# Spreading the adaLN row sums differently over the two passes of a SwiGLU's second matrix

## The chip, the cores and the metric

The kernel runs on one core of one Trainium2 chip. The metric is the device time of one execution in microseconds; the median of three timed runs of the kernel before is 2384.79 us (2383.39 to 2386.68).

## What is computed

Two layers, each a macaron block: a SwiGLU half step (FFN), a mixing step (attention, a chunked gating MLP and pooling), and a second FFN. That makes six stages: 0, 2, 3 and 5 are FFNs, 1 and 4 mix. Each stage ends with a gated residual and leads into a modulated norm; gate, scale and shift are the adaLN rows, each one a vector times a 1024 x 1024 slice of `w_mod`.

```python
def adaln(cvec, w_mod_l, b_mod_l):
    m = jax.nn.silu(cvec) @ w_mod_l + b_mod_l
    return m.reshape(cvec.shape[0], N_MOD, D_MODEL)
def ffn_half(x, mod, j, g_pre, g_post, w1, w2):
    h = modulate(rms_norm(x, g_pre), mod, j)
    return x + 0.5 * mod[:, j + 2][:, None, :] * rms_norm(swiglu(h, w1, w2), g_post)
```

There are 640 tokens (512 latent, 128 context), D_MODEL = 1024, D_FF = 2816, all in float32; context and latent tokens have their own conditioning vector, so every adaLN row is computed for two vectors.

## The kernel before, in words

**Precision.** Every operand of a large matmul is split into a rounded high part (ScalarE copy) and a low part (VectorE subtraction), and a product is three matmuls: hi x hi, lo x hi, hi x lo. For weights this is line 329 (`whi`, ScalarE) and line 331 (`wlo`, VectorE), for activations of the second matrix lines 765 (`ahi`) and 766 (`alo`).

**Tiles.** The five token tiles of 128 are in two groups: group A has tiles 0 and 1, group B tiles 2, 3 and the context tile 4. `ffn1` and `ffn1_blocks` compute the first matrix; its results are `act[f, g]` for 22 slices f of 128 hidden columns. `ffn2` computes the second matrix in two passes: the first pass for group A, the second for group B. A pass goes through 22 slices f and two output halves, that is 44 weight units of 128 x 512; each is loaded by a DMA on SyncE's queue (line 283, tile `raw`, five buffers) and split. The second pass keeps the last four units of the first and loads 40. In `mm_tok` (line 700) a unit yields 650 ns of nominal time per tile: 44 x 2 x 650 ns = 57.2 us for the first pass, 44 x 3 x 650 ns = 85.8 us for the second. The last four slices of a first pass are done tile by tile, so that tile 0 is complete before the pass ends. The products of tiles 0 and 1 stand in PSUM banks 4 to 7, those of tiles 2, 3 and 4 in banks 0 and 1, 2 and 3, 4 and 5.

**Boundary.** After a pass, `boundary` (`bnd_steps`, line 489) closes the stage for its tiles: square sums (ScalarE, 498), product with the gate row `mdG` (VectorE, 499), residual (509, or 506 in the last stage), norm (512), scale and shift rows (517 on VectorE, 520 on GpSimd), eight transposes a tile (528) and splits for the next stage (361, 362). Group A's boundary runs beside the second pass, group B's beside the start of the next stage. In stage 5 it ends at 506 and writes the output.

**adaLN rows.** `ada` (line 418) computes a list of rows in the background. A row takes a zeroed tile with the bias (`wb`, GpSimd 424, DMA 425), eight loads of 512 KB of `w_mod` (line 431, tile `wmt`, three buffers shared with `wb` and `gr`), for each of these two VectorE operations on 128 x 1024 (line 436, one for each conditioning vector, 16 a row), four DMAs of `norm_w` (442), four matmuls with ones that add over the partitions (445; the trace shows eight records), one operation that scales (449, 451 or 453), and four DMAs that write the row to DRAM (457). `load_md` (460) reads it back later, spread over all partitions. `rows(n)` gives the rows that the end of stage n wants: its gate G, and for the next stage S and T; stage 5 wants a gate alone. A row's yields are 8 x (300 + 2 x 1150) + 1700 = 22.5 us of nominal time.

**What sets the order.** The program is written as generators. `run` (122) and `beside` (137) step a main generator and let a background generator advance by a rate times the main one's nominal time. So a rate is a share of nominal time, and it fixes where in the order of the program the row's operations stand; `behind` moves them back by 30 places of priority. A scheduler then orders each engine's instructions by priority and a simulated timeline; on the chip each engine and each DMA queue works through its list in that order.

Stage s runs the rows of `ADA_LATE[s]` in its second matrix, in both passes at `ADA_RATE2`. In stage 0 six more rows run earlier, beside `ffn1`; that part is not touched.

```python
ADA_LATE = {0: (2,), 2: (3,), 3: (4, 5), 5: ()}
ADA_RATE2 = 0.7
...
            bg = ada(rows[1])
            run(self.ffn2(l, i, 0), (bg, ADA_RATE2))
            self.rings(ada=(7,))
            self.second_pass(s, last, self.ffn2(l, i, 1, last), bg)
```

`ffn2` splits activations with `ensure` (756): the first slice before its first matmul, then two slices ahead. The tiles come from pool `asp`, which in stages 2, 3 and 5 (`BLOCKS`) is opened only after `ffn1_blocks`, in memory that the tiles `SZ` of those blocks held.

Of the kernel before, what the change touches and what calls it, by code (L numbers as in the profile page):

```python
# [8 lines left out]
F32 = mybir.dt.float32  # L9
F32R = mybir.dt.float32r  # L10
# [5 lines left out]
P = 128  # L16
D = 1024
KD = 8
FF = 2816
NF = 22  # L20
# [5 lines left out]
WA = 256  # L26
# [4 lines left out]
ADA_LAG = 30  # L31
ADA_RATE = 0.65

ADA_LATE = {0: (2,), 2: (3,), 3: (4, 5), 5: ()}
ADA_RATE2 = 0.7

BLOCKS = (2, 3, 5)
S_LAG, S_RATE = 400, 0.45
# [112 lines left out]
def drain(*gens):  # L151
    for g in gens:
        for _ in g:
            pass
# [7 lines left out]
class Builder:  # L162
    def __init__(self, ctx, tc, a, n_stage=6):
# [32 lines left out]
        self.rowd = {}  # L196
        self.pairs = {}
        self.gap = None
        self.kept_tmp = {}

    def bank(self, i):
# [498 lines left out]
    def mm_tok(self, key, tiles, order, stat, late=0, tail=1):  # L700
# [18 lines left out]
        while ci < n:  # L719
# [25 lines left out]
                    yield 650 * len(tiles)  # L745
            ci += 1

    def ffn2(self, l, i, g, last=False):
        wid = (WA, WB)[g]
        sp = {}  # L750

        order = list(range(NF))
        if g:
            order = order[NF - KEEP_C:] + order[:NF - KEEP_C]

        def ensure(f):
            while len(sp) <= min(f, NF - 1):
                q = order[len(sp)]
                hi = self.asp.tile([P, WB], F32R, name="ahi")
                a = self.act[q, g]  # L760
                if len(sp):
                    lo = self.ap.tile([P, wid], F32, name="alo", tag=f"act{g}{order[len(sp) - 1]}").bitcast(F32R)
                else:
                    lo = self.asp.tile([P, WB], F32R, name="ahi")[:, 0:wid]
                self.nc.scalar.activation(hi[:, 0:wid], a, AF.Copy)  # L765
                self.nc.vector.tensor_tensor(lo, a, hi[:, 0:wid].bitcast(F32), ALU.subtract)  # L766
                sp[q] = (hi, lo)

        def stat(f):
            ensure(order.index(f) + 2)  # L770
            return sp[f]
        ensure(0)
        yield from self.mm_tok(lambda c, n: ("w2", l, i, c, n), (GA, GB)[g], order, stat, late=1 if g else 0, tail=(TAIL_A, TAIL_B, TAIL)[g + last])
# [523 lines left out]
    def ffn_stage(self, s, l, i, pend):  # L1297
# [8 lines left out]
        with tc.tile_pool(name="gap", bufs=1, reuse_waits="tile") as gp, tc.tile_pool(name="actp", bufs=1, reuse_waits="tile") as ap, ExitStack() as late:  # L1306
# [19 lines left out]
            if s in BLOCKS:  # L1326
                with tc.tile_pool(name="sp", bufs=2, reuse_waits="tile") as sp:
# [7 lines left out]
                    run(self.ffn1(l, i, early[-1:], (1,)))  # L1335
                    self.sum_in_place()
                    self.rings(acc=(0, 1, 2, 3, 4, 5, 6, 7))
                    run(self.ffn1_blocks(l, i, range(na, NF)))
            if s in BLOCKS:
                pools()  # L1340
            ada = lambda rows: behind(tc, self.ada(rows, block(self.wmp, "wmt"), block(self.accsp, "acc")), ADA_LAG)
# [12 lines left out]
                self.load_md(kind, s)  # L1354
            self.rings(ada=(3,))
            bg = ada(rows[1])
            run(self.ffn2(l, i, 0), (bg, ADA_RATE2))
            self.rings(ada=(7,))
            self.second_pass(s, last, self.ffn2(l, i, 1, last), bg)
            for t in (3, 4):  # L1360
# [3 lines left out]
    def second_pass(self, s, last, mm, bg=None):  # L1364
        q = STG[s]
        if bg:
            mm = beside(mm, bg, ADA_RATE2)
        b = self.boundary(s, GA, True, not last, 1, q["skew_a"])
        next(b)
        next(b)  # L1370
# [84 lines left out]
```

## Time and profile before

| | before |
|---|---|
| median of three runs | 2384.79 us |
| the profiled execution's own time | 2385.23 us |
| span of the profile | 2383.5 us |
| PE, DVE, ACT, POOL busy | 97%, 77%, 47%, 17% of the span |
| granted TensorE clock, mean | 0.993 of 2.4 GHz |

PE is TensorE's matmul stream, PEld its weight loads, DVE VectorE, ACT ScalarE, POOL GpSimd, SPq the DMA queue of SyncE. Busy shares are means over stages with different limits; matmul records overlap, so how long a stretch took says more than how busy PE was in it. An instruction's duration is longer than its share of a full engine, since the next one starts before it ends.

### The profile page before, as it was taken

To read this page: it belongs to the slowest core of one execution; us is meant where nothing else is said; L and a number is where in the kernel's file an instruction comes from. 1 tells how busy PE (TensorE), PEld (TensorE's weight loads), DVE (VectorE), ACT (ScalarE), POOL (GpSimd) and SP (SyncE) were. 2 spreads that over 40 slices of the span, in tenths; PEclk is the share of its full clock that TensorE was granted. 3 is DMA by queue.
4 is the path that set the end of the run, shared out by engine and by line. 5 is a ranking of instruction groups with operands and counts; after the bars stand their busy time and mean duration, and the time that the engine had idled before them with its cause. 6 is when DMAs were issued, how large, how long until landed. Compare 5 with 4: busy or idle time off the path is not lost.

```text
span 2383.5 us, 37305 instructions
## 1 busy us (share of the span) xinstructions
PE 2300.2 (97%) x13304; PEld 2050.9 (86%) x13304; DVE 1827.1 (77%) x2914; ACT 1118.5 (47%) x2309; POOL 393.5 (17%) x432
## 2 busy tenths in 40 slices
PE   8999999999999999998999999999999989999998
PEld 6999897787778899996789999877777779999887
DVE  5568678977686788889976888899867674888754
ACT  5422224444776344454443444444555553444543
POOL 2000000305324200000240000020645360000000
PEclk9999999999999999999999999999999999999999
DMA  9457657644325522247653322667621354232542
GB/s 295 117 174 244 200 189 261 232 157 137 98 72 168 160 85 84 80 160 248 222 181 120 89 86 75 212 227 244 204 74 63 106 173 134 75 89 71 187 158 93
DMA packets 330481, 360.07 MB, mean 151 GB/s; under 512 B 20451, under 2 KB 239843, under 8 KB 330294
## 3 DMA queue, kind: packets, MB, share of 16 engines
q1 hardware_dynamic: 326694, 344.58, 45.5%
q10 hardware_dynamic: 3600, 13.11, 1.4%
q8 instruction: 104, 1.70, 0.3%
q14 instruction: 83, 0.68, 0.1%
HBM read 341.50 MB, written 16.12 MB: 150 GB/s over the span
## 4 chain that ended last, share of the span: by engine, by line
PE 71%; DVE 13%; DMA 6%; issue 5%; POOL 2%; ACT 2%; SPq 1%; DVEq 0%; ACTq 0%; POOLq 0%
PE PS L366 69%; DVE wlo L331 3%; DMA wmt<-in_w_mod 3%; DVE acc L436 3%; DMA raw<-in_ffn_w 2%; DVE alo L766 1%; PE PS L445 1%; POOL tmp L520 1%; DVE ast L1063 1%; DVE x L509 1%; PE PS L1086 1%; DVE tl L362 1%; DVE h1lo L362 1%; POOL wlo L331 1%; ACT whi L329 0%
## 5 line engine op out<-in xcount | busy, mean ns | idle before, releaser
L329 ACT ACTIVATE whi<-raw 128x512 fp32r<-128x512 f32 x668 | 416.5, 630 | 525.5 <-PE PS L366 379.5
L331 DVE TENSOR_TENSOR wlo<-raw,whi 128x512 fp32r<-128x512 f32 x614 | 455.2, 755 | 198.7 <-ACT whi L329 190.0
L366 PE MATMUL PS<-whi,ahi 128*128 128x512 f32 x920 | 353.6, 392 | 0.0
L366 PE MATMUL PS<-h1hi,whi 128*128 128x384 f32 (+1 forms) x1016 | 341.5, 337 | 6.4 <-ACT h1hi L361 6.4
L366 PE MATMUL PS<-h1lo,whi 128*128 128x384 f32 (+1 forms) x1016 | 344.6, 339 | 0.0
L366 PE MATMUL PS<-wlo,ahi 128*128 128x512 f32 x880 | 342.7, 391 | 0.0
L366 PE MATMUL PS<-h1hi,wlo 128*128 128x384 f32 (+1 forms) x1016 | 341.8, 336 | 0.0
L329 ACT ACTIVATE whi<-tmp 128x512 fp32r<-128x512 f32 x294 | 185.7, 633 | 244.6 <-PE PS L366 175.3
L436 DVE SCALAR_TENSOR_TENSOR acc<-wmt,ccs,acc 128x1024 f32<-128x1024 f32 x224 | 279.9, 1279 | 26.8 <-DMA wmt<-in_w_mod 26.7
L366 PE MATMUL PS<-h0hi,whi 128*128 128x256 f32 x1016 | 287.3, 284 | 7.6 <-DVE act L602 7.4
L366 PE MATMUL PS<-whi,alo 128*128 128x512 f32 x840 | 272.7, 395 | 21.2 <-DVE alo L766 20.9
L366 PE MATMUL PS<-h0hi,wlo 128*128 128x256 f32 x1016 | 285.4, 282 | 0.0
L366 PE MATMUL PS<-h0lo,whi 128*128 128x256 f32 x1016 | 285.3, 281 | 0.0
L331 DVE TENSOR_TENSOR wlo<-tmp,whi 128x512 fp32r<-128x512 f32 x294 | 201.7, 687 | 77.5 <-ACT whi L329 71.4
L366 PEld LDWEIGHTS PS<-whi,alo 128*128 128x128 f32 x840 | 155.3, 188 | 66.6 <-DVE alo L766 30.0
L366 PEld LDWEIGHTS PS<-h0hi,whi 128*128 128x128 f32 x1016 | 193.5, 191 | 18.4 <-DVE act L602 8.8
L366 PEld LDWEIGHTS PS<-whi,ahi 128*128 128x128 f32 x920 | 173.8, 189 | 39.1 <-ACT ahi L765 1.7
L366 PE MATMUL PS<-sz,whi 128*128 128x384 f32 x784 | 199.3, 335 | 0.0
L366 PEld LDWEIGHTS PS<-h0hi,wlo 128*128 128x128 f32 x1016 | 193.6, 191 | 4.3 <-issue 3.4
L366 PEld LDWEIGHTS PS<-h1hi,whi 128*128 128x128 f32 x1016 | 190.7, 188 | 7.0 <-ACT h1hi L361 7.0
L366 PEld LDWEIGHTS PS<-wlo,ahi 128*128 128x128 f32 x880 | 166.2, 189 | 34.7
L366 PEld LDWEIGHTS PS<-h0lo,whi 128*128 128x128 f32 x1016 | 193.9, 191 | 1.8 <-issue 1.7
(239 smaller groups left out, 4204.6 us busy)
## 6 DMA issues: line engine op xcount, KB each, us to landing
raw<-in_ffn_w SPq DMA_DIRECT2D x540, 256.0 KB
wmt<-in_w_mod SPq DMA_DIRECT2D x136, 512.0 KB
tmp<-in_ffn_w SPq DMA_DIRECT2D x98, 512.0 KB
raw<-in_w_in SPq DMA_DIRECT2D x80, 256.0 KB
xd<-x ACTq DMA_DIRECT2D x25, 512.0 KB
x<-xd SPq DMA_DIRECT2D x25, 512.0 KB
raw<-in_w_out SPq DMA_DIRECT2D x64, 128.0 KB
mdG<-rowG SPq DMA_DIRECT2D x12, 512.0 KB
```

The source lines that it names most:

```text
L329: self.nc.scalar.activation(hi, r, AF.Copy)
L331: eng.tensor_tensor(lo, r, hi.bitcast(F32), ALU.subtract)
L362: i1 = (eng or self.nc.vector).tensor_tensor(lo, src, hi.bitcast(F32), ALU.subtract)
L366: self.nc.tensor.matmul(out, w, m, start=start, stop=stop)
L436: nc.vector.scalar_tensor_tensor(accs[s], w, self.cc[:, s, k:k + 1], prev, ALU.mult, ALU.add)
L445: nc.tensor.matmul(ps[32 * q:32 * q + 32, :], self.ones[:, 0:32], accs[q // 2][:, 512 * (q % 2):512 * (q % 2) + 512], start=True, stop=Tru ...
L509: nc.vector.scalar_tensor_tensor(x, tmp, r, x, ALU.mult, ALU.add)
L520: nc.gpsimd.tensor_tensor(tmp[:, hs], tmp[:, hs], self.md["T", st][:, hs], ALU.add)
L766: self.nc.vector.tensor_tensor(lo, a, hi[:, 0:wid].bitcast(F32), ALU.subtract)
L1063: nc.vector.tensor_reduce(mx, S, AX.X, ALU.max)
L1086: nc.tensor.transpose(ps[:, w * c + P * j:w * c + P * j + P], pt[:, n * j + P * (c0 + c):n * j + P * (c0 + c) + P], self.ident)
```

## The change

Three edits. First, the two passes get rates of their own: 0.3 in the first and 0.62 in the second pass of stages 0, 2 and 3 in place of 0.7 in both. Second, the one row of stage 5 (its gate) moves from the end of stage 3's list into stage 5's own first pass, at rate 0.5; what is left of it is issued when that pass is written out, and then its two `load_md` DMAs. Third, in stages 2, 3 and 5 the high and low parts of group A's slices 0 and 1 are made ahead of the last slice of `ffn1_blocks`, into a tile of the `tmp` pool, and `ffn2` takes them from there.

```diff
-ADA_LATE = {0: (2,), 2: (3,), 3: (4, 5), 5: ()}
-ADA_RATE2 = 0.7
+ADA_LATE = {0: (2,), 2: (3,), 3: (4,), 5: (5,)}
+ADA_RATES = {0: (0.3, 0.62), 2: (0.3, 0.62), 3: (0.3, 0.62), 5: (0.5, 0.62)}
...
+    def split_first(self):
+
+        t = self.tmpp.tile([P, D], F32, name="first", tag="tmp").bitcast(F32R)
+        self.early = {}
+        for f in range(2):
+            hi, lo = (t[:, 512 * f + WA * n:512 * f + WA * n + WA] for n in range(2))
+            self.split(hi, lo, self.act[f, 0])
+            self.early[f] = (hi, lo)
+
     def ffn2(self, l, i, g, last=False):
         wid = (WA, WB)[g]
         sp = {}
+        if g == 0 and self.early:
+            sp, self.early = self.early, {}
...
-                    run(self.ffn1_blocks(l, i, range(na, NF)))
+                    run(self.ffn1_blocks(l, i, range(na, NF - 1)))
+                    self.split_first()
+                    run(self.ffn1_blocks(l, i, range(NF - 1, NF)))
...
-            run(self.ffn2(l, i, 0), (bg, ADA_RATE2))
+            run(self.ffn2(l, i, 0), (bg, ADA_RATES[s][0]))
+            if last:
+                drain(bg)
+                self.load_md("G", s)
             self.rings(ada=(7,))
...
-            mm = beside(mm, bg, ADA_RATE2)
+            mm = beside(mm, bg, ADA_RATES[s][1])
```

## Rows read from the trace of the kernel before

**Rows 1.** The page's first line.

```profile
span 2383.5 us, 37305 instructions
```

**Rows 2.** Windows, the passes of stages 0, 2, 3, 5: length, busy us, clock, DMA share, GB/s.

```profile
364.30:430.87 66.57, 63.26 (x274) 49.42 (x273) 60.05 (x84) 30.29 (x58) 0.95 (x1) 1.00 0.79 261
430.87:530.85 99.98, 97.42 (x430) 77.45 (x429) 82.78 (x105) 46.88 (x88) 20.40 (x16) 0.98 0.56 185
1054.37:1124.38 70.01, 63.48 (x273) 49.36 (x273) 63.39 (x90) 31.03 (x59) 0.95 (x1) 1.00 0.83 281
1124.38:1222.33 97.95, 95.08 (x431) 76.09 (x430) 80.78 (x103) 46.24 (x88) 16.57 (x15) 1.00 0.58 189
1515.58:1584.69 69.11, 63.90 (x273) 49.36 (x273) 61.25 (x88) 30.82 (x59) 0.96 (x1) 1.00 0.83 286
1584.69:1684.91 100.22, 97.62 (x430) 77.34 (x429) 97.91 (x118) 47.06 (x88) 21.96 (x16) 0.98 0.68 228
2227.21:2287.09 59.88, 59.88 (x265) 49.57 (x265) 39.45 (x68) 32.77 (x66) 0.86 (x2) 1.00 0.60 198
2287.09:2377.01 89.92, 89.92 (x397) 74.16 (x395) 43.94 (x69) 35.16 (x68) 2.59 (x6) 1.00 0.35 119
```

**Rows 3.** Waits of PE over the span: total us, times, longest.

```profile
PE PS L366 <- DVE alo L766: 20.9, 17, 2.3
```

**Rows 4.** Windows of line 436 alone, DVE: a first pass, stage 3's second, after.

```profile
364.30:430.87 66.57, 30.28 (x25) 1.00 0.79 261
...
1584.69:1684.91 100.22, 48.76 (x39) 0.98 0.68 228
1684.91:1695.00 10.09, 1.27 (x1) 1.00 0.55 181
```

**Rows 5.** Timeline of DVE in stage 0's first pass: start us, us.

```profile
397.19 2.48 DVE L436 SCALAR_TENSOR_TENSOR acc<-wmt,ccs,acc 128x1024 f32<-128x1024 f32 x2
...
399.92 1.29 DVE L331 TENSOR_TENSOR wlo<-raw,whi 128x512 fp32r<-128x512 f32 x2
```

**Rows 6.** Windows of line 445 alone, PE then PEld: one row, two rows.

```profile
364.30:430.87 66.57, 2.10 (x8) 0.29 (x8) 1.00 0.79 261
...
1584.69:1684.91 100.22, 2.85 (x16) 0.45 (x16) 0.98 0.68 228
```

**Rows 7.** Windows, ends of second passes: stage 0 without rows, stage 3 with.

```profile
495.50:530.85 35.35, 35.35 (x160) 28.58 (x160) 18.61 (x30) 16.23 (x31) 1.25 (x3) 1.00 0.45 142
...
1650.00:1684.91 34.91, 34.91 (x159) 28.43 (x152) 33.05 (x42) 16.12 (x31) 1.63 (x2) 1.00 0.80 263
```

**Rows 8.** Timelines of POOL, DVE and PE in stage 3's second pass.

```profile
1606.40 6.88 POOL L520 TENSOR_TENSOR tmp<-tmp,mdT 128x512 f32<-128x512 f32 x4
...
1608.69 3.47 DVE L331 TENSOR_TENSOR wlo<-raw,whi 128x512 fp32r<-128x512 f32 x2
...
1613.75 1.73 PE L366 MATMUL PS<-whi,alo 128*128 128x512 f32 x5 [1.82 <-DVE alo L766]
```

**Rows 9.** Timeline of PE after stage 2's second pass.

```profile
1243.97 0.38 PE L366 MATMUL PS<-h0hi,whi 128*128 128x256 f32 x1 [1.84 <-DVE act L602]
```

**Rows 10.** Timelines of PE and SPq: from a row's matmuls to its loads.

```profile
403.16 2.25 PE L445 MATMUL PS<-acc,ones 128*32 128x512 f32 x8
...
407.95 0.56 SPq L457 DMA_DIRECT2D rowG<-wmt  x2
...
177.16 1.13 SPq L457 DMA_DIRECT2D rowG<-wmt  x4
...
180.63 0.90 SPq L465 DMA_DIRECT2D mdG<-rowG  x2
```

**Rows 11.** Timeline of DVE at the end of stage 5's first pass.

```profile
2282.57 0.69 DVE L499 TENSOR_TENSOR tmp<-PS,mdG 128x512 f32<-128x512 f32 x1 [4.72 <-ACT mk L498]
```

**Rows 12.** Timelines of ACT and PE where stage 2's first pass begins.

```profile
1053.03 1.02 ACT L765 ACTIVATE ahi<-act 128x256 fp32r<-128x256 f32 x3
...
1054.37 0.39 PE L366 MATMUL PS<-whi,ahi 128*128 128x512 f32 x1
```

More of the change, by code (lines that the diff above doesn't have):

```diff
@@ L746, in mm_tok @@
             ci += 1
+    def split_first(self):
+        t = self.tmpp.tile([P, D], F32, name="first", tag="tmp").bitcast(F32R)
+        self.early = {}
+        for f in range(2):
+            hi, lo = (t[:, 512 * f + WA * n:512 * f + WA * n + WA] for n in range(2))
+            self.split(hi, lo, self.act[f, 0])
+            self.early[f] = (hi, lo)
     def ffn2(self, l, i, g, last=False):
```

## The prediction

> **What bounds the kernel now.** The page's first line gives the span [rows 1]; the profiled execution took 2385.23 us, so 1.73 us lie around it. I cut the second matrices out of the trace by PE's timeline: a pass runs from its first to its last product. The table of windows is what decides [rows 2]. Stage 5 has no adaLN work and is the yardstick: its passes take 59.88 and 89.92 us, PE is never idle in them, and DVE has much room (39.45 and 43.94 us busy). The same products take 66.57, 70.01 and 69.11 us in the first passes of stages 0, 2 and 3 and 99.98, 97.95 and 100.22 us in the second ones. DVE is there at 60 to 63 us of 67 to 70, and in stage 3's second pass at 97.91 of 100.22. The list of waits says what PE lacks: low parts of activations, 20.9 us in 17 waits [rows 3]. So it is DVE in these passes: a row's multiply-adds stand in its queue ahead of `alo` and `wlo`.
>
> The excess of the three first passes is 205.69 - 3 x 59.88 = 26.0 us. One adaLN row ends in each, and its summing matmuls take PE 2.10 us [rows 6]; that leaves 26.0 - 6.3 = 19.7 us of stalls. The excess of the three second passes is 298.15 - 3 x 89.92 = 28.4 us: two rows each (2.85 us in stage 3, [rows 6]), the transposes of the boundary, and stalls.
>
> **The change, part by part.**
>
> *Rates.* Nominal times first. Before, the first pass brought 0.7 x 57.2 = 40.0 of a row's 22.5, so 1.8 rows; the rest of three rows, 27.5, took 27.5 / 0.7 = 39 of the second pass's 85.8, and the rest of stage 3's four rows, 50, took 71. After, the first pass brings 0.3 x 57.2 = 17.2, which is 0.76 row or 13 multiply-adds instead of 25 [rows 4], and no row ends there. The other 50.3 take 50.3 / 0.62 = 81 of 85.8, so a second pass gets 48 - 13 = 35 multiply-adds and three row ends. Before it had 23 or 24, in stage 3 39 and one more after it [rows 4].
>
> *First passes.* Two multiply-adds back to back take 2.48 us [rows 5], so one costs DVE 1.2 us. DVE without them needs 60.05 - 30.28 = 30 us in stage 0 [rows 2, 4] to 39.45 in stage 5, which already starts its boundary; 13 more make 45 to 55 us in a pass of 60. That is under PE, where before it was above: the old rate asked for some 31 multiply-adds in the pass's nominal time, 37 us, and with 30 to 32 that is 67 to 69 us, which is how long the passes became. I take 60.5 us a pass: the yardstick and 0.6 us for short bursts. Bounds: no stall at all (59.9), or half of the 19.7 us left (63.2 us). Sum: 3 x 60.5 - 205.7 = -24.2 us, between -26 and -16.
>
> *Second passes.* One row end more: by [rows 6] 1.4 us in each, +4.2. DVE: stage 2's second pass has 80.78 us with 23 multiply-adds; 12 more and a row end make about 96 us, in a pass that PE alone holds for 97 to 99. That is full, but stage 3 has shown it with 39 (97.91 of 100.22), and its last 35 us show that a full queue need not cost PE anything: DVE 33.05 and PE 34.91 of 34.91; without rows the same stretch of stage 0 leaves DVE at 18.61 [rows 7]. So the added work goes into an empty half, and the stalls that are there stay. The largest of them stays by its cause: four GpSimd additions of the boundary take 6.88 us, two `wlo` beside them take 3.47 us where two take 1.29 elsewhere, and PE then waits 1.82 us for `alo` [rows 5, 8]; stages 0 and 2 show the same. The mean clock of 0.98 in two of the passes [rows 2] is a short drop to 1.2 GHz behind that wait. The Trainium skill, SBUF — State Buffer (Who interferes with whom), says that a VectorE operation with two SBUF inputs and a GpSimd operation that reads SBUF lock each other out of a shared port. By that rule no rate gets rid of these stalls; if they were overload alone, some 5 us more would go and the sum would be about 2367 us. The rows side with the rule. I take 0 for the stalls, between -6 (overload gone in the boundary) and +9 (3 us more in each, since DVE is full for longer).
>
> *The ends of second passes.* Rows are now issued up to 95% of the pass, and DVE needs 96 of some 99 us, so the last row's end spills over, as stage 3's fourth does now (last multiply-add after 1684.91, [rows 4]). For stage 3 this changes little, and its fourth row goes: -2.1 us of PE [rows 6], no longer behind the pass. In stages 0 and 2 it is new. After stage 2 PE waits for DVE already (1.84 us, [rows 9]), so two late operations tell there; the start of a mixing stage has products to go on with. I take +1.5 us, between 0 and +8.
>
> *Stage 5's own gate row.* 2.1 us of PE. At rate 0.5 its operations are issued over 45 of the first pass's 57.2; there DVE has about 39.45 x 0.79 + 16 x 1.2 + 0.7 = 51 us in 47, a little over full, against 67 to 69 in 60 for the old rate. The old overload of 13% cost 4 to 8 us a pass, so for this one, shorter and smaller, I take 3 us, between 0 and 6. The wait that is added: line 499 of group A's boundary now waits for the gate's loads, and behind it in DVE's queue stand the `alo` and `wlo` of the second pass. The row's matmuls come at about 52 us of a pass of 65 (47, PE's 3 us of stalls, and the lag of 2 us that the first row in stage 0 shows: 403.16, where 32.1 of 57.2 nominal falls at 401.7, [rows 10]); from matmuls to the last write of the row it takes 5 us, from the writes to the loads' issue 3.5 [rows 10]; for landing I reckon with 3 to 4, bounds 2 and 7. So the gate is there at 63 to 65 us, where line 499 first needs it 55 us into the pass as it is now (2282.57 of 2227.21, [rows 11]) and it hurts from about 61 + the pass's own stalls. SyncE's queue is quiet there: it has issued the pass's weights. I take +2 us, between 0 and 10. Sum for stage 5: +7.1.
>
> *Early splits.* Nothing: in stage 2 the three `ahi` start 1.34 us before the first product that needs one, and that product follows the block's last with no wait [rows 12]. The same copies and subtractions move into a block where ACT and DVE have idle time. Between -0.5 and +0.5.
>
> Sum: -24.2 + 4.2 + 0 - 2.1 + 1.5 + 7.1 = -13.5. 2385.23 - 13.5 = 2371.7 us; the median of the runs is 0.4 below the profiled one, so this is no offset that matters. What I call no change is 0.2% of the median, 4.8 us: 2380.0 to 2389.6.
>
> **The rivals.**
>
> *Transfers hold the first passes.* The DMA share is 0.79 to 0.83 there and 0.60 in stage 5 [rows 2]; a first pass with 0.76 row moves nearly as many bytes a us as stage 0's does now. If weights landing late were the cause, half of the 24 us stays: 2371.7 + 10 = 2382. Against it: PE's waits are for `alo`, which needs no transfer [rows 3], and DVE is over 90% busy.
>
> *The gate row comes late.* If stage 5's row takes the pace that rows have in the full second passes, it is 10 us later, line 499 holds DVE, and PE stands for nearly all of that: 2381. For it: the queue order is fixed and DVE is in order. Against: the first rows of the passes come close to their nominal place.
>
> *The spill decides: slower.* Rows issued at 95% of a full pass end 10 us behind it if DVE's backlog is that of stage 3 now, where the fourth row was issued up to 83% and ended 4 us past the pass. Then some eight multiply-adds stand among group B's boundary, which is on PE's path after stage 2. Price: 10 us there and 5 after stages 0 and 3, +20: 2392 us. It decides from some 4 us of multiply-adds past the pass. Against: DVE's sum of 96 us fits, and stage 3's 39 did.
>
> *More than forecast.* Boundary stalls shrink by 6 us and stage 5 costs 3 instead of 7: 2362.
>
> *The change doesn't do what it says* holds for the early splits alone, and costs nothing.
>
> **How the numbers follow.** Forecast 64%, more 8%, transfers 10%, late gate 10%, spill 8%. The predicted time is the forecast's, 2371.7. Its own range from the bounds, not all at one end, is 2364 to 2379. The range that holds 8 in 10 goes down to the better case, 2361, and up past the transfers and the late gate, 2383. Faster: nearly all of forecast and better (0.71) and less than half of the two middle cases, 0.77. Slower: the spill, 0.07. Within 0.2%: the rest, 0.16.
>
> **What would show it.** First passes of stages 0, 2 and 3 at 60 to 61.5 us with 12 to 14 multiply-adds and no line 445; second passes at 98 to 101 us with about 35, DVE over 93 us, and the slow pair of `wlo` beside GpSimd still there; the last line 436 of these stages within 4 us of the pass's end; stage 5's first pass at 64 to 66 us, with line 499 released by a DMA of `mdG`. I am wrong if first passes stay over 64 us (transfers), if stage 5's two passes together grow by over 10 us (gate), or if multiply-adds run well into the next stage and PE's gaps after stage 2 grow (spill).

## The result, and the profile after

The changed kernel takes 2408.15 us (median of 4 runs, 2406.20 to 2410.63); the kernel before, on the same chip, 2384.09. The ratio is 1.0099, with a 95% interval of 1.0084 to 1.0114: slower by 1%, where I had forecast 2371.7 us and a range of 2361 to 2383. The profiled execution took 2406.94 us. Line numbers in the changed kernel are higher by one up to the middle of the file: 331 is 332 (`wlo`), 436 is 437 (the multiply-adds), 445 is 446 (a row's matmuls), 499 is 500, 766 is 778 (`alo`).

The first line and one group of the page. In the group, the last part is the idle time of the engine just before these instructions, and what ended it. The first two lines are of the changed kernel, the last is the same group before.

```profile
span 2405.1 us, 37322 instructions
...
L437 DVE SCALAR_TENSOR_TENSOR acc<-wmt,ccs,acc 128x1024 f32<-128x1024 f32 x224 | 280.7, 1282 | 66.6 <-DMA wmt<-in_w_mod 66.4
...
L436 DVE SCALAR_TENSOR_TENSOR acc<-wmt,ccs,acc 128x1024 f32<-128x1024 f32 x224 | 279.9, 1279 | 26.8 <-DMA wmt<-in_w_mod 26.7
```

As many multiply-adds as before, of the same length, but VectorE stands idle for 40 us more ahead of them, for the load of `wmt`.

The windows of the eight passes, which answer to [rows 2]: window, length, busy us (instructions) of PE, PEld, DVE, ACT, POOL, clock, DMA share, GB/s.

```profile
364.06:431.08 67.02, 61.64 (x266) 49.16 (x265) 45.14 (x70) 31.11 (x65) 0.00 (x0) 1.00 0.57 193
431.08:533.76 102.68, 98.73 (x430) 77.97 (x429) 92.20 (x112) 43.35 (x81) 16.11 (x16) 0.97 0.65 219
1067.67:1137.28 69.61, 63.54 (x266) 50.22 (x265) 47.05 (x73) 30.55 (x63) 0.00 (x0) 0.98 0.66 227
1137.28:1239.73 102.45, 100.05 (x439) 77.39 (x438) 97.24 (x119) 44.51 (x82) 16.93 (x16) 0.98 0.65 216
1531.87:1602.02 70.15, 64.67 (x265) 51.48 (x265) 47.39 (x74) 30.87 (x63) 0.00 (x0) 0.95 0.67 231
1602.02:1701.69 99.67, 97.58 (x430) 77.27 (x429) 90.71 (x111) 43.20 (x81) 16.57 (x16) 0.98 0.66 220
2246.47:2308.77 62.30, 62.30 (x273) 49.69 (x273) 51.17 (x78) 31.32 (x63) 0.87 (x2) 1.00 0.80 264
2308.77:2398.70 89.93, 89.92 (x397) 74.16 (x395) 46.70 (x75) 35.17 (x68) 3.65 (x6) 1.00 0.36 123
```

The windows of line 437 alone: two passes and the stretches behind second passes, which answer to [rows 4]. (A window counts each instruction that overlaps it, so one on the edge of two windows is counted in both.)

```profile
364.06:431.08 67.02, 14.88 (x12) 1.00 0.57 193
...
1137.28:1239.73 102.45, 44.12 (x36) 0.98 0.65 216
...
533.76:560.00 26.24, 3.80 (x3) 0.93 0.56 181
...
1701.69:1720.00 18.31, 4.45 (x3) 0.91 0.62 189
```

The reader is to see a paradox. All that the change was to do to the first passes, it did: 12 to 14 multiply-adds instead of 25, no row end (266 matmuls, not 274), VectorE busy for 45 to 47 us instead of 60 to 63. The passes are as long as before all the same: 67.0, 69.6 and 70.2 us. Where the span's 21.6 us come from (after minus before, by PE's passes; the differences are rounded last):

| part | before | after | measured | forecast |
|---|---|---|---|---|
| first passes of stages 0, 2, 3 | 205.7 | 206.8 | +1.1 | -24.2 |
| second passes of stages 0, 2, 3 | 298.1 | 304.8 | +6.7 | +4.2 |
| end of stage 0's pass to stage 2's first pass | 523.5 | 533.9 | +10.4 | |
| end of stage 2's pass to stage 3's first pass | 293.2 | 292.1 | -1.1 | |
| end of stage 3's pass to stage 5's first pass | 542.3 | 544.8 | +2.5 | |
| the three stretches together | 1359.1 | 1370.8 | +11.8 | -0.6 |
| stage 5's passes | 149.8 | 152.2 | +2.4 | +7.1 |
| before the first pass and after the last | 370.7 | 370.5 | -0.3 | 0 |

VectorE's waits in stage 0's first pass (who, line, for what: us in all, times, longest), then PE's, each in the changed kernel and then before:

```profile
DVE acc L437 <- DMA wmt<-in_w_mod: 15.1, 5, 3.5
...
DVE acc L436 <- DMA wmt<-in_w_mod: 5.7, 6, 3.3
```

```profile
PE PS L367 <- DVE wlo L332: 5.4, 4, 2.2
...
PE PS L366 <- DVE alo L766: 3.1, 3, 1.2
```

PE now waits for `wlo`, and before it waited for `alo`; in the first passes of stages 2 and 3 it waits for `wlo` too, 5.4 and 5.5 us. Now the same pass of the changed kernel in the timelines (start, length, engine, line, operation; in brackets the idle time ahead and who ended it): VectorE, then ScalarE, then SyncE's queue, then PE.

```profile
398.41 0.42 DVE L778 TENSOR_TENSOR alo<-act,ahi 128x256 fp32r<-128x256 f32 x1
402.35 2.48 DVE L437 SCALAR_TENSOR_TENSOR acc<-wmt,ccs,acc 128x1024 f32<-128x1024 f32 x2 [3.52 <-DMA wmt<-in_w_mod]
404.75 1.29 DVE L332 TENSOR_TENSOR wlo<-raw,whi 128x512 fp32r<-128x512 f32 x2
...
413.24 2.48 DVE L437 SCALAR_TENSOR_TENSOR acc<-wmt,ccs,acc 128x1024 f32<-128x1024 f32 x2 [2.54 <-DMA wmt<-in_w_mod]
...
423.62 2.48 DVE L437 SCALAR_TENSOR_TENSOR acc<-wmt,ccs,acc 128x1024 f32<-128x1024 f32 x2 [3.13 <-DMA wmt<-in_w_mod]
...
431.85 3.68 DVE L437 SCALAR_TENSOR_TENSOR acc<-wmt,ccs,acc 128x1024 f32<-128x1024 f32 x3 [4.22 <-DMA wmt<-in_w_mod]
435.45 0.68 DVE L500 TENSOR_TENSOR tmp<-PS,mdG 128x512 f32<-128x512 f32 x1
```

```profile
397.98 0.62 ACT L330 ACTIVATE whi<-raw 128x512 fp32r<-128x512 f32 x1
```

```profile
396.05 0.42 SPq L432 DMA_DIRECT2D wmt<-in_w_mod  x1
396.56 10.77 SPq L284 DMA_DIRECT2D raw<-in_ffn_w  x6
407.38 0.42 SPq L432 DMA_DIRECT2D wmt<-in_w_mod  x1
...
418.27 0.42 SPq L432 DMA_DIRECT2D wmt<-in_w_mod  x1
```

```profile
405.49 0.50 PE L367 MATMUL PS<-wlo,ahi 128*128 128x512 f32 x1 [1.59 <-DVE wlo L332]
...
426.75 0.50 PE L367 MATMUL PS<-wlo,ahi 128*128 128x512 f32 x1 [2.24 <-DVE wlo L332]
...
436.19 0.55 PE L367 MATMUL PS<-whi,ahi 128*128 128x512 f32 x1 [3.13 <-DVE tmp L500]
```

A load is issued at 396.05; its multiply-adds start at 402.35, when it has landed, but VectorE came to them 3.52 us earlier, and the first `wlo` at 404.75 has to stand behind them, though its `whi` was done at 398.60. PE runs dry until 405.49. The next loads are issued at 407.38 and 418.27, their multiply-adds start 5.9 and 5.4 us later, and each time PE waits for `wlo` behind them. At 431.85 it hits the start of the second pass: the boundary's line 500 stands behind three multiply-adds, and PE waits 3.13 us for it.

### The profile page after: what moved, and what is told of

Its sections match the earlier page's. It is cut to its first block, busy times and chain, and to the rows that moved or that the text cites. A ratio compares the mean times of both kernels' runs of the same rounds, so it can differ in the third digit from the quotient of the medians.

```text
span 2405.1 us, 37322 instructions
## 1 busy us (share of the span) xinstructions
PE 2314.1 (96%) x13304; PEld 2059.2 (86%) x13304; DVE 1830.7 (76%) x2914; ACT 1112.4 (46%) x2309; POOL 381.0 (16%) x432
## 4 chain that ended last, share of the span: by engine, by line
PE 76%; DVE 9%; DMA 5%; issue 4%; POOL 3%; ACT 2%; SPq 1%; DVEq 0%; ACTq 0%; POOLq 0%
PE PS L367 73%; DMA raw<-in_ffn_w 3%; DVE wlo L332 2%; DVE acc L437 2%; DMA wmt<-in_w_mod 2%; PE PS L446 1%; POOL tmp L521 1%; DVE ast L1075 1%; PE PS L1098 1%; ACT whi L330 1%; POOL wlo L332 1%; PE PS L529 0%; DVE h1lo L363 0%; DVE tl L363 0%; DVE alo L778 0%
## 5 line engine op out<-in xcount | busy, mean ns | idle before, releaser
L367 PE MATMUL PS<-whi,ahi 128*128 128x512 f32 x884 | 346.0, 399 | 8.4 <-DVE tmp L500 8.3
L437 DVE SCALAR_TENSOR_TENSOR acc<-wmt,ccs,acc 128x1024 f32<-128x1024 f32 x224 | 280.7, 1282 | 66.6 <-DMA wmt<-in_w_mod 66.4
L367 PE MATMUL PS<-whi,alo 128*128 128x512 f32 x828 | 318.3, 395 | 0.6 <-DVE alo L778 0.6
L425 POOL MEMSET wmt<- 128x1024 f32 x16 | 15.3, 955 | 1398.8 <-PE PS L367 777.3
L367 PEld LDWEIGHTS PS<-h1lo,whi 128*128 128x128 f32 x1016 | 190.8, 188 | 3.3 <-issue 1.7
```

The lines of the kernel that those rows point to most:

```text
L367: self.nc.tensor.matmul(out, w, m, start=start, stop=stop)
L425: nc.gpsimd.memset(wb, 0.0)
L437: nc.vector.scalar_tensor_tensor(accs[s], w, self.cc[:, s, k:k + 1], prev, ALU.mult, ALU.add)
```

## The experiments

All times are medians; each kernel was run in turn with the kernel before on one chip, which gave 2380.7 to 2385.8 us there. The last four columns are PE's first passes of stages 0, 2 and 3 and the sum of their second passes.

| run | us | ratio to before (95%) | first passes | | | second |
|---|---|---|---|---|---|---|
| e6_split_alone | 2385.11 | 1.0003 (0.9992, 1.0014) | 66.4 | 65.0 | 66.3 | 308.6 |
| e1_old_rates | 2383.20 | 0.9993 (0.9984, 1.0003) | 67.1 | 66.9 | 68.8 | 305.5 |
| e2_stage0_old | 2395.10 | 1.0043 (1.0027, 1.0058) | 66.5 | 66.4 | 72.1 | 301.0 |
| e3_load_ahead | 2375.93 | 0.9959 (0.9944, 0.9974) | 62.5 | 61.2 | 63.9 | 298.9 |
| e4_before_load_ahead | 2373.70 | 0.9948 (0.9931, 0.9965) | 67.6 | 66.6 | 67.2 | 291.7 |
| e5_second_08 | 2398.25 | 1.0055 (1.0034, 1.0076) | 68.9 | 66.3 | 68.3 | 311.2 |
| e7_ahead_second_08 | 2370.56 | 0.9942 (0.9923, 0.9960) | 62.5 | 61.3 | 62.5 | 307.1 |
| e8_ahead_free | 2378.67 | 0.9972 (0.9960, 0.9984) | 66.1 | 65.2 | 64.6 | 291.0 |
| e9_no_load_wait | 2372.28 | 0.9947 (0.9930, 0.9965) | 66.1 | 65.4 | 65.0 | 296.2 |
| e10_no_row_end | 2400.44 | 1.0064 (1.0047, 1.0081) | 69.0 | 70.3 | 70.7 | 301.4 |
| e11_ahead_old_rates | 2374.43 | 0.9953 (0.9938, 0.9968) | 67.3 | 66.5 | 66.4 | 293.9 |
| e12_ahead_mid_rates | 2379.05 | 0.9975 (0.9965, 0.9986) | 61.1 | 65.1 | 64.9 | 306.3 |
| e13_ahead_paced | 2357.93 | 0.9897 (0.9878, 0.9916) | 59.9 | 59.9 | 59.9 | 290.0 |
| e14_ahead_paced_08 | 2354.18 | 0.9879 (0.9859, 0.9900) | 59.9 | 59.9 | 59.9 | 296.3 |
| e15_paced_only | 2396.18 | 1.0058 (1.0036, 1.0081) | 66.9 | 65.9 | 67.2 | 302.1 |
| e16_old_rates_paced | 2371.34 | 0.9956 (0.9941, 0.9971) | 65.5 | 66.6 | 66.4 | 294.5 |

### The parts of the change by themselves

**Early splits alone** (old rates, gate row at its old place):

```
-ADA_LATE = {0: (2,), 2: (3,), 3: (4,), 5: (5,)}
+ADA_LATE = {0: (2,), 2: (3,), 3: (4, 5), 5: ()}
-ADA_RATES = {0: (0.3, 0.62), 2: (0.3, 0.62), 3: (0.3, 0.62), 5: (0.5, 0.62)}
+ADA_RATES = {0: (0.7, 0.7), 2: (0.7, 0.7), 3: (0.7, 0.7), 5: (0.7, 0.7)}
...
-                drain(bg)
-                self.load_md("G", s)
```

> The early splits alone, rates and rows as before. My theory puts none of the changed kernel's 24 us here: the three ahi of stage 2 stood 1.3 us ahead of their product already, so 2384 +- 2 us, and the 24 matmuls on the early tile start without a wait. Rival: the early tile takes a buffer of the tmp pool from the block's combined weights and holds up the last block: each of stages 2, 3 and 5 loses 2 us or more at its end, 2390 us.

They are worth nothing, 1.0003. Behind that zero the first passes of stages 2 and 3 are 5.0 and 2.8 us shorter and the second ones 6.1 and 3.2 longer: the work shifts, the pair keeps its length to within 1.1 us.

**Old rates, all else as changed:** the line of `ADA_RATES` reads `{0: (0.7, 0.7), 2: (0.7, 0.7), 3: (0.7, 0.7), 5: (0.5, 0.7)}`.

> The changed kernel with 0.7 in both passes of stages 0, 2 and 3; the last gate row stays in stage 5 and the early splits stay. Theory (the loss comes from the new rates: spill behind the passes, and first passes that wait for row loads): the 24 us go, stage 5's first pass stays 2.4 us longer, stage 3's end loses its fourth row, so 2383 to 2387 us. Rival (the gate row in stage 5 or the moved order costs it): 2395 us or more.

2383.20: the rates carry all of the loss (25 us against the changed kernel), the moved gate row and the splits together none, as the theory had it. That zero is a sum as well: against the kernel before, the second passes are 7.3 us longer (10.5 with the splits alone) and the first ones 3.0 shorter. Stage 4 starts its work 7.8 us sooner here (534.5 us instead of 542.3 from stage 3's last product to stage 5's first): the fourth row, which spilled over stage 3's end before, is gone.

**Old rates in stage 0 alone:** `{0: (0.7, 0.7), 2: (0.3, 0.62), 3: (0.3, 0.62), 5: (0.5, 0.62)}`.

> The changed kernel with the old rate 0.7 in stage 0 alone. Theory (the spill of stage 0's last row into the start of the mixing stage costs 10 us there, besides 3 us in the second pass): 13 us less than the changed kernel, 2395 us, with stage 1's first 40 us as in the kernel before. Rival (a diffuse loss, a third of it from each of the three stages): 8 us less, and stage 1's start still 5 us or more behind; rival (nothing to do with stage 0's rows): 2408 us.

2395.10, the theory's time. Stage 0's second pass (97.8) and the stretch behind it (523.9, as before) give back some 15 us; its first pass is 66.5, with VectorE's load waits down to 3.3 us. So at the old rate the first pass is held by overload, at the new one by late loads, and both come to the same length.

### Loads one step ahead, and denser second passes

```
+            ws = []
+            def load(k):
+                ws.append(wt())
+                with self.after(self.gate_dma):
+                    nc.sync.dma_start(ws[k], src[:, k, :])
+            load(0)
             for k in range(KD):
-                w = wt()
-                with self.after(self.gate_dma):
-                    nc.sync.dma_start(w, src[:, k, :])
+                if k + 1 < KD:
+                    load(k + 1)
+                w = ws[k]
```

> The changed kernel with each of a row's eight loads issued one step earlier in the program: load k+1 stands ahead of the multiply-adds of load k, in the same three buffers. Theory (first passes gained nothing because VectorE, with its queue no longer backed up, reaches a multiply-add before its load has landed and stands there with wlo and alo behind it): VectorE's waits for row loads in the first pass of stage 0 fall from 15 us to under 4, the three first passes fall from 67, 70, 70 to 61 to 63 us, and the kernel to 2385 to 2392 us, with the spill in stage 1 still there. Rival (transfers hold the passes: weights land late because the DMA engines are busy): first passes stay at 66 us or more and the kernel at 2403 us or more.

2375.93, better than either side of the expectation, by a mechanism only half right. VectorE's waits for loads, in the changed kernel with this edit, stage 0's first pass:

```profile
DVE acc L444 <- DMA wmt<-in_w_mod: 9.2, 5, 3.9
```

They did not go away (9.2 us; 13.7 with the one at the second pass's start), but most are shorter, and PE pays for one of them only (2.2 us). So it is not the sum of the waits that costs PE; it looks to be each one that outlasts what PE has in stock.

**The same edit in the kernel before:**

> The kernel before with the row loads issued one step earlier, old rates and rows. Theory (with 0.7 VectorE is overloaded in the first passes and seldom waits for loads, 5.7 us in stage 0's first pass, so the earlier issue helps only once the rate is lower): the first passes stay within 3 us of 66.6, 70.0 and 69.1 us, 2378 to 2386 us. Rival (the earlier issue is all of the gain that the changed kernel with loads ahead has over the kernel before, and the lower rate adds nothing): first passes at 61 to 64 us and 2376 us or less.

2373.70, less than the 2378 to 2386 that the theory gave, and the rival's time: a gain that needs nothing of the change. The rival's first passes of 61 to 64 us did not come: they fall little (67.6, 66.6, 67.2; 4.3 us together), and PE waits there for `alo` as before, so overload holds those. The second passes get 6.5 us shorter together.

**Second passes at 0.8** (`(0.3, 0.8)` in stages 0, 2 and 3), without and with the loads ahead:

> The changed kernel with 0.8 instead of 0.62 in the second passes of stages 0, 2 and 3, so that rows are issued up to 73% of the pass. Theory (rows' ends that spill behind the pass cost 10 us at the start of stage 1): the last multiply-add of stage 0 comes before the pass's end, the stretch from there to stage 2's second matrix falls from 533.9 to about 524 us, and the kernel to 2396 to 2401 us; first passes stay at 67 to 70 us. Rival (the loss at stage 1's start has another cause, or it only moves into the second passes, which grow by as much): 2405 us or more.

> Loads one step ahead, and 0.8 in the second passes. Theory: both losses of the changed kernel go, the late loads and the spill; against the kernel with loads ahead alone (2376 us) the 5.5 us that stage 1 still loses at its start go, so 2369 to 2373 us. Rival (a full VectorE at the boundary gives it back in the second passes): 2376 us or more.

2398.25 and 2370.56, both within the theory's range. In both no multiply-add comes behind a pass any more, and the stretch behind stage 0 is 526.7 and 525.1 us instead of 533.9 and 529.0, behind stage 3 it is 540.3 and 534.9. What the spill gives, the second passes take in part (311.2 and 307.1 us).

### Waits for loads taken away altogether

**Loads ahead and no longer tied to the place of the weights' loads** (`self.free` is true while rows laid over a second matrix are issued):

```
+                with nullcontext() if self.free else self.after(self.gate_dma):
+                    nc.sync.dma_start(ws[k], src[:, k, :])
```

> Loads one step ahead as before, and in the second matrix without the order that puts each row load behind the latest weight load in SyncE's queue. Theory (a row load comes late because in SyncE's queue it stands behind weight loads that wait for a free buffer): loads are issued 8 us or more ahead of their multiply-add instead of 5, VectorE's waits for them in stage 0's first pass fall from 13.7 us to under 5, and the first passes to 60 to 62 us; 2366 to 2374 us. Rival (the loads are slow because the DMA engines are busy, whenever they are issued, and then hold up weights instead): waits on weights grow, 2376 us or more.

**Multiply-adds of second-matrix rows read the row's bias tile in place of the loaded weights:**

```
-   nc.vector.scalar_tensor_tensor(accs[s], w, self.cc[:, s, k:k + 1], prev, ALU.mult, ALU.add)
+   nc.vector.scalar_tensor_tensor(accs[s], wb if self.free else w, self.cc[:, s, k:k + 1], prev, ALU.mult, ALU.add)
```

> The changed kernel in which the multiply-adds beside the second matrix read the row's bias tile in place of the loaded slice of w_mod; the loads are still issued, at the same places, but nothing waits for them (the rows computed there are left out of the result). Theory (multiply-adds that wait in VectorE's in-order queue for a load issued about 3 us before are what keeps the first passes long, and with one of them line 500 and tile 4's banks at the start of the second passes): VectorE's waits for loads go to 0, the first passes of stages 0, 2 and 3 fall from 67, 70, 70 to 60 to 62 us, the second passes by 2 to 5 us, and the kernel to 2365 to 2380 us; the spill at the mixing stages' start may stay. Rival (the pace of the weights, held by the DMA engines and the row loads between them): first passes stay at 66 us or more, the kernel at 2400 us or more.

In both VectorE waits for no load in that pass, and the first passes are 65 to 66 us, not 60 to 62: a miss, and it made me doubt the theory. The first run takes 2378.67, above its 2366 to 2374; the second, 2372.28, is within its range for all that its first passes are not. The reason is in VectorE's order. Nothing holds these multiply-adds back any more, so they are moved forward: in stage 0's first pass 16 of them come within 35 us of its start, PE waits for `alo` again (4.6 us in 5 waits in the one, 4.7 in the other), which is what the overload of the kernel before looked like. By this reading the rate in the source did not set the pace, the load did; the runs with a held pace, below, test it.

**No row end behind stage 0** (the multiply-adds of its third row stay; its matmuls, copy and writes go, and the next row's data stand in):

```
+            if (kind, n) == ("T", 2):
+                self.rowd[kind, n] = self.rowd[kind, 1]
+                continue
```

> The changed kernel without the end of stage 0's last row: its 16 multiply-adds and its loads stay, but its norm loads, four matmuls, scaling and the four writes are left out (a row of an earlier stage is loaded in its place, so the result differs). Theory (stage 1 loses its 10 us at the start because the row's late write holds SyncE's queue and the memory that the mixing stage's tiles take over): most of it goes, the stretch from the second pass's end to stage 2's second matrix falls from 533.9 to 524 to 527 us, the kernel to about 2400 us. Rival (it is the late multiply-adds that push group B's boundary back on VectorE): the stretch falls by less than 3 us.

The stretch behind stage 0 falls from 533.9 to 529.7, against 523.5 before: 4.2 of the 10.4 us belong to the row's end. That lies between the theory (524 to 527) and the rival (less than 3 us). The other 6.2 are left to the late multiply-adds and the boundary behind them, which this run does not part.

**Loads ahead at the old rates, and at rates between** (`(0.45, 0.75)` in the three stages):

> Loads one step ahead, the last gate row in stage 5, early splits, and the old rate 0.7 in both passes of stages 0, 2 and 3. Theory (the fourth row of stage 3 cost 8 us at stage 4's start in the kernel before, and the earlier loads shorten the second passes at any rate): against the kernel before with loads ahead (2373.7 us) 8 us less at stage 4 and 2.4 us more in stage 5, 2366 to 2370 us. Rival (the lower rates are what lets the moved gate pay): 2373 us or more.

> As the last one with 0.45 in the first and 0.75 in the second pass. Theory: first passes at 61 to 64 us as with 0.3, the last row ends some 20 us inside the second pass, so no spill in stages 1 and 4, and second passes at 98 to 101 us: 2362 to 2369 us, the fastest of these. Rival (what the first pass saves the second gives back, so the sum of the two passes does not depend on the rate): the two passes of stages 0, 2 and 3 together stay at 163 us or more each, 2370 us or more.

2374.43 and 2379.05. With the loads ahead alone the rates are worth nothing (2375.93 at the new ones), and the middle is worse than both: 61.1 us in stage 0's first pass, but 104.6 in its second, and the pairs of passes stay at 165.7 to 166.0 us, as the rival had it. With the old rates (e11) the 8 us at stage 4 came in part (535.6 us against 541.2 in e4), but stage 5's first pass grew by 5.3 us instead of 2.4 and took them back.

### Early loads and a held pace

To have early loads without a denser pace, each multiply-add was also ordered behind the newest `wlo` of VectorE at its place in the program:

```
-            eng.tensor_tensor(lo, r, hi.bitcast(F32), ALU.subtract)
+            split = eng.tensor_tensor(lo, r, hi.bitcast(F32), ALU.subtract)
+            if eng is self.nc.vector:
+                self.pace = split
...
-                    with self.after(self.gate):
+                    with self.after(self.gate), self.after(self.pace) if self.free else nullcontext():
```

> Loads one step ahead as in the run before of that kind (2375.93), and each multiply-add of the adaLN rows laid over a second matrix is also ordered behind the newest VectorE split (wlo) at its place in the program, so that it can't be brought forward. Theory (what holds the first passes at 66 to 70 us is a multiply-add that waits for its load at the head of VectorE's queue; with the load early and the low pace kept, nothing is left): VectorE's waits for wmt in stage 0's first pass fall under 4 us (15.1 in the changed kernel, 13.7 with the load ahead alone), the first passes of stages 0, 2 and 3 go to 60 to 62 us, the spill in front of stages 1 and 4 stays, and the time is 2362 to 2372 us. Rival (something other than load waits and pace holds these passes): the first passes stay at 63 us or more and the time is 2375 us or more.

> The changed kernel with the multiply-adds ordered behind the newest VectorE split as in the two others, but each load still issued just before its multiply-add. Theory: the pace is the same and the loads are late as before, so VectorE's waits for wmt in stage 0's first pass stay at 10 us or more, the first passes of stages 0, 2 and 3 at 66 us or more, and the time is 2398 us or more. Rival (the pace alone does it, the load's place does not matter): these passes fall to 63 us or less and the time to 2385 us or less.

2357.93 with the loads ahead, 4 us under the theory's range, and 2396.18 with the loads where the change has them. The two kernels differ in the place of the loads alone. VectorE's waits in stage 0's first pass, in the one and in the other:

```profile
DVE acc L447 <- DMA wmt<-in_w_mod: 1.3, 1, 1.3
```

```profile
DVE acc L440 <- DMA wmt<-in_w_mod: 18.1, 6, 4.1
```

The windows of the one with early loads, stages 0 and 2 (columns as above):

```profile
364.54:424.40 59.86, 59.86 (x266) 49.55 (x265) 52.63 (x78) 32.39 (x65) 2.91 (x3) 1.00 0.70 230
424.40:519.78 95.38, 95.38 (x430) 76.33 (x429) 87.60 (x107) 43.13 (x81) 13.68 (x14) 1.00 0.69 228
1047.94:1107.82 59.88, 59.88 (x265) 49.55 (x265) 53.50 (x80) 31.59 (x63) 2.78 (x3) 1.00 0.78 271
1107.82:1206.98 99.16, 99.16 (x439) 76.53 (x438) 90.18 (x112) 43.71 (x83) 12.72 (x13) 1.00 0.68 221
```

This settles the first passes. With 16 multiply-adds in the pass, more than the changed kernel's 12, PE is full for 59.86 of 59.86 us, the yardstick of stage 5 without a row [rows 2]. Stage 3's takes 59.88. Same pace with late loads: 65.9 to 67.2. The theory of the late loads expected 2398 or more there; 2396.18 is a little less, the direction is the same.

**The same at 0.8 in the second passes:**

> The same, with 0.8 in place of 0.62 as the second passes' rate, so that the rows end inside the passes. Theory: first passes as in the other, no spill in front of stage 1 (525 us from the second pass's end to stage 2, against 529 to 534 with it) nor stage 4, and the time is 2358 to 2367 us. Rival (what the second passes take on they give back): the second passes are 3 us or more longer each than in the other, and the time is 2370 us or more.

2354.18, the fastest of all and 4 us under the theory's range, 1.2% below the kernel before; its lead over 2357.93 is within what two intervals leave open (0.9859 to 0.9900 against 0.9878 to 0.9916). No multiply-add spills, and the stretches behind stages 0 and 3 fall to 523.4 and 535.6 us (528.2 and 544.1 at 0.62); the second passes take 6.4 us of that back, which is the rival's part.

**And at the old rates:**

> Loads ahead and paced multiply-adds as in the two last runs (2357.93 with 0.3 and 0.62, 2354.18 with 0.3 and 0.8), with the old rates 0.7 and 0.7 in stages 0, 2 and 3. It tells what the change's thinner first passes are worth once no multiply-add waits for its load. Theory (my forecast's mechanism: at 0.7 VectorE's work is longer than the pass, at 0.3 it isn't): the first passes are 65 us or more, the time is 2365 to 2375 us. Rival (early loads and pace alone give the gain, whatever the rates): first passes of 62 us or less and a time of 2360 us or less.

2371.34, with first passes of 65.5, 66.6 and 66.4 us, as the theory had it. So the change's thinner rate is worth 13.4 us where the loads are early and the pace is held, and costs 25 where neither is so:

| medians, us | old rates | new rates |
|---|---|---|
| loads late | 2383.20 (e1) | 2408.15 (the change) |
| loads late, pace held | | 2396.18 (e15) |
| loads ahead | 2374.43 (e11) | 2375.93 (e3) |
| loads ahead, pace held | 2371.34 (e16) | 2357.93 (e13) |

## Why the prediction was wrong

**The step that failed** is the first passes: "That is under PE, where before it was above", and from it 60.5 us a pass. I showed that VectorE's work fits, and took that for proof that PE would be full. VectorE works its queue in order, and a load was issued 300 ns of nominal time ahead of its multiply-adds, so 1 us of pass at 0.3, while it takes some 5 to 6 us from issue to use. Before, VectorE's own backlog gave the loads that time; the change removed the backlog and so the cover. In the trace before, a load of the same pass takes as long: the one below has its multiply-adds at 397.19 [rows 5], 5.9 us later, and VectorE comes to them without an idle moment. Of this pass's 13 loads, 12 were met with 0.7 us of idle time or less.

```profile
391.26 0.42 SPq L431 DMA_DIRECT2D wmt<-in_w_mod  x1
```

I asked of every other edit what hides it, and not of the loads. The trace of before had the sign: 26.8 us of idle time ahead of line 436, and 5.7 us of it in stage 0's first pass. This one term is 25 of the 35 us between the forecast and the profiled execution; the spill below is 12 more, and stage 5 gave 5 back.

**The rival that transfers hold the first passes** had the place right and the cause half: it is not bytes (the pass ran at a mean DMA share of 0.57, and e13 moves 230 GB/s there in place of 193), but when a load is issued. I argued against it with what PE waits for before ([rows 3], `alo`), which tells what binds now and not what binds next.

**Second passes:** +6.7 for +4.2, with the parts wrong. A row end more came in stage 2 alone; in stages 0 and 3 the third row ends behind the pass. The multiply-adds were 33, 35 and 31 (by where they start) for 35, VectorE was busy for 92.2, 97.2 and 90.7 us. PE was idle for 8.4 us in the three passes, before for 8.0 (length less busy, above and in [rows 2]), but for another reason: the waits for `alo` went, and the waits for line 500 at the start of the passes, behind multiply-adds that wait for loads, came; in stage 0 they are shown above at 431.85 and 436.19. The mean clock was 0.97, 0.98 and 0.98 where it had been 0.98, 1.00 and 0.98.

**The stalls "that are there stay"** was wrong. I had weighed the Trainium skill, SBUF — State Buffer (Who interferes with whom), by which a VectorE operation with two SBUF inputs and a GpSimd operation that reads SBUF shut each other out. The pair is still there in the changed kernel, POOL and VectorE in stage 0's second pass:

```profile
447.50 6.91 POOL L521 TENSOR_TENSOR tmp<-tmp,mdT 128x512 f32<-128x512 f32 x4
```

```profile
449.79 3.48 DVE L332 TENSOR_TENSOR wlo<-raw,whi 128x512 fp32r<-128x512 f32 x2
453.19 1.64 DVE L778 TENSOR_TENSOR alo<-act,ahi 128x384 fp32r<-128x384 f32 x1
```

Two `wlo` take 3.48 us, before 3.47 [rows 8], so the rule and the trace agree on VectorE's time. But PE has no wait after it. What follows the pair on VectorE is not the reason, since before, too, `alo` came next behind the pair, and PE waited 1.82 us [rows 8]:

```profile
1612.09 1.61 DVE L766 TENSOR_TENSOR alo<-act,ahi 128x384 fp32r<-128x384 f32 x1
```

In e16, at the old rates, the wait is back, and there two multiply-adds stand between; VectorE, then PE:

```profile
1596.84 3.48 DVE L333 TENSOR_TENSOR wlo<-raw,whi 128x512 fp32r<-128x512 f32 x2
1600.25 3.50 DVE L447 SCALAR_TENSOR_TENSOR acc<-wmt,ccs 128x1024 f32<-128x1024 f32 x2
1603.67 0.54 DVE L788 TENSOR_TENSOR alo<-act,ahi 128x384 fp32r<-128x384 f32 x1
```

```profile
1604.27 1.65 PE L370 MATMUL PS<-whi,alo 128*128 128x512 f32 x6 [2.28 <-DVE alo L788]
```

What differs is how much stands ahead of the pair: between the second pass's start and the four GpSimd additions there are six or seven multiply-adds before, five or six in e16, two to four in the changed kernel and none in e13. So the slow pair costs PE time only where VectorE comes to it late; that fits these traces, but no run tests it by itself. In the three second passes together PE waited for `alo` for 7.8 us before and not at all in the changed kernel, where I had taken these stalls to stay. With early loads and held pace the second passes are 8.2 us shorter than before (290.0 for 298.1), with the row end more in stage 2 alone; in e14, where all three passes have it, they are 1.8 us shorter.

**The spill:** +11.8 for -0.6, in other places than I looked. Behind stage 2, where I feared it, nothing is lost. Behind stage 0 it costs 10.4, 9.9 of it by the next stage's 60th product, which starts 27.0 us after the pass's end. The timelines there, VectorE, ACT and PE:

```profile
535.11 1.26 DVE L437 SCALAR_TENSOR_TENSOR acc<-wmt,ccs,acc 128x1024 f32<-128x1024 f32 x1
...
538.32 1.26 DVE L437 SCALAR_TENSOR_TENSOR acc<-wmt,ccs,acc 128x1024 f32<-128x1024 f32 x1
...
540.71 1.27 DVE L510 SCALAR_TENSOR_TENSOR x<-tmp,r,x 128x1024 f32<-128x1024 f32 x1
541.90 1.27 DVE L437 SCALAR_TENSOR_TENSOR acc<-wmt,ccs,acc 128x1024 f32<-128x1024 f32 x1
```

```profile
542.01 1.06 ACT L513 ACTIVATE tmp<-x 128x1024 f32<-128x1024 f32 x1 [6.41 <-DVE x L510]
```

```profile
543.23 1.05 PE L446 MATMUL PS<-acc,ones 128*32 128x512 f32 x4 [1.66 <-DVE acc L437]
545.02 0.50 PE L367 MATMUL PS<-whi,h0hi 128*128 128x512 f32 x1 [0.75 <-ACT wmt L450]
...
555.66 0.56 PE L367 MATMUL PS<-whi,h0hi 128*128 128x512 f32 x1 [2.18 <-DVE pl L901]
```

Group B's residual (line 510) starts 6.95 us after the pass's end, behind two multiply-adds that come after that end, and a third stands ahead of the residual's next part; before it started just ahead of the end, at 530.28 of 530.85. ACT waits 6.41 us for it, with the next weights' `whi` behind, and PE has little to go on with. The rival "the spill decides" had this mechanism, and 20 us as its price. What I held against it ("stage 3's 39 did") was a bad comparison: stage 3 of before, with one multiply-add behind its pass [rows 4], was paying itself. Without its fourth row and without a spill that stretch takes 534.5 (e1) to 535.6 (e14) instead of 542.3. Behind stage 3 the change thus lost the 7.8 us that the moved row had freed (544.8 for 542.3). How these parts divide among late multiply-adds, row end and boundary is known for stage 0 alone (e10).

**Stage 5's gate row:** +2.4 us for +7.1. The wait came where I put it, but costs PE nothing. VectorE at the pass's end, which answers to [rows 11]:

```profile
2308.46 1.29 DVE L500 TENSOR_TENSOR tmp<-PS,mdG 128x512 f32<-128x512 f32 x2 [6.75 <-DMA mdG<-rowG]
```

The gate is there 62.0 us into a pass of 62.3, so just in time; PE is never idle in either pass. The 3 us of stalls that I took for the small overload did not come either. The 3 to 4 us that I reckoned for landing stood on no row; here line 500 starts 4.0 us after the issue of the first of the two loads (2304.45). **Early splits:** 0, as forecast.

A word on the near hit of the mechanism: e13 against e16 gives -13.4 us, and my sum was -13.5. That is luck: my sum also held the moved gate row, which both of these runs have, and the terms differ. The first passes are -18.9 (I had -24.2, from longer ones), the second passes -4.5 for +4.2, and the spill is +11 for +1.5.

## What to carry to other kernels

Before work is spread thinner on an in-order engine, ask for each operation that waits for a transfer what gives the transfer its time now; if it is the engine's own backlog, thinning removes it, and the loads have to be issued earlier in the same edit. Here that alone was not enough: the loads had to be early and the multiply-adds held to their pace. That the busy sum fits the window does not show that nothing waits: look at the idle time ahead of the moved operation in the trace of before, and at what stands behind it in the queue. Where the program's order is not the order on the engine, a rate in the source is a wish, and an explicit order after a neighbour made it hold.

## What the runs showed of the hardware

A 512 KB load of `wmt` took from its issue on SyncE to the start of its multiply-adds 6.3, 5.9 and 5.4 us in the changed kernel's first pass of stage 0, and VectorE stood idle for the last 3.5, 2.5 and 3.1 of them. The pass's DMA share of 0.57 is a mean that hides how the transfers came: it was 0.86, 0.87 and 0.92 while these three loads were under way beside loads of weights, and 0.20 and 0.36 between them. So the passes did not lack transfer time, they had it in bursts. Not each wait costs the same: that of 3.52 us at 402.35 cost PE 1.59, that of 3.13 at 423.62 cost 2.24.

The granted clock was 0.98 and 0.95 in the changed kernel's first passes of stages 2 and 3, so partly at 1.2 GHz, and 1.00 (2.4 GHz) in the same passes of e13, where PE is never idle. In stage 2 it stood at 1.2 GHz from 1132.8 to 1136.2, shortly after PE's longest wait of that pass (3.14 us, up to 1131.35). So some of what the passes lost was clock and not waiting; that PE's idle time brought the clock down is not shown by a run of its own.
